# A hybrid encoder layer on one core: the gates of four heads and the forget logits of two heads computed as one more 2x2 block group

## The chip, the cores and the metric

The kernel runs on one core of one Trainium2 chip. The metric is the device time in microseconds. Five engines work side by side, each through its own queue of instructions in a fixed order, and they wait for each other by semaphores: TensorE (PE, matrix products), VectorE (DVE), ScalarE (ACT), GpSimd (POOL) and SyncE (SP, which issues most of the transfers). A matrix product reads its operands from the on-chip memory and adds into one of eight banks of 512 fp32 columns; DVE and ACT read those banks. An instruction that has to wait holds up everything behind it on its engine.

## The reference

One layer on x of 256 tokens by 2048 channels, all in fp32: half a feed-forward block, a mixer, half a feed-forward block. Only the mixer matters here:

```
h = rms_norm(x, pre_norm_mix)
q_h, i_h, f_fwd, f_bwd, g_h, q_a, k_a, v_a = split(h @ w_mix_in)  # 1024 columns each, k_a and v_a 256
qh, vh = heads(q_h), heads(i_h)                                   # 8 heads of 128
f = lb + (1 - lb) * sigmoid(heads(f_logit)); log_f, k = log(f), 1 - f   # forward, and backward flipped
o = chunk_scan(qh, k, vh, log_f)                                  # the two directions are added
y_h = o * rsqrt(mean(o * o) + EPS) * out_gain * silu(g_h)         # per head
y_a = window_attention(q_a, k_a, v_a, sink, rel_table)
x = x + rms_norm(concat(y_h, y_a) @ w_mix_out, post_norm_mix)
```

The columns of `w_mix_in` are, in this order, queries of the recurrence (0 to 1023), values (1024 to 2047), forward forget logits (2048 to 3071), backward forget logits (3072 to 4095), gates (4096 to 5119), queries of the attention (5120 to 6143), keys and values of the attention (6144 to 6655).

## The kernel before

**How fp32 products are made.** A weight tile is loaded from memory as a raw tile of 128 partitions by 2048 columns and split into halves of 1024 columns: ACT writes the rounded part `h` (line 177), DVE the remainder `l = raw - h` (line 178). The tokens `xt` have been split in the same way. A product in full precision is three passes on PE (line 458): `h` by high tokens, `l` by high tokens, `h` by low tokens. The tiles `h` and `l` come from two pools of five, so a new half can be written when PE is done with the half five before it. Three raw tiles are kept.

**Three forms of a projection.** *Values*: the 1024 value columns are a group of 2x2 blocks. `c` is four banks (token half m, column half n), and the 2048 input channels are eight pairs of 128. A plain pair takes eight products in three passes, 24 instructions. A pair of the class's table goes by seven products instead of eight (Strassen's scheme in Winograd's form): 21 instructions, into four further banks `p1, p5, p6, p7`, with sums of blocks made before. For the weights these sums are two accumulating transfers' work (issued by POOL, which adds block rows into the raw tile) and two DVE additions; for the tokens `sum_up` makes them. A raw tile of such a pair lies in one half of a room of its own, `vr`, and not in the three raw tiles. After the last mixed pair, `fold` adds the `p` banks into the `c` banks. *Gates* (`gates`, lines 379 to 381): 16 channel tiles by two token halves by three passes, 96 instructions of 512 columns per 512 gate columns. *Head pairs* (`headpair`, lines 326 and 331): 256 columns, weights stationary, so that the result stands with columns on partitions, which the recurrence needs: 32 instructions of 512 columns (high and low tokens at once) and 32 of 256 columns.

**The order.** Values, then for each pair of heads hp = 0 to 3: forward forget logits `zf`, backward `zb`, queries `q`, attention queries `qa`, each a `headpair`. The gates of heads 0 to 3 stand in hp = 1 between `zf` and `zb`. Small work of the recurrence and the attention is handed out between the pieces of the head pairs, by the generators in `side`: every `yield n` lets n pieces pass. Eight pieces are one half of a head pair. The values' part is written in a manual schedule: PE, DVE and ACT execute in the order of the text. Outside it a scheduler sets the order, by the text too, but with freedom.

Of the kernel before, what the change touches and what calls it, by code (L numbers as in the profile page):

```python
# [37 lines left out]
def hymba_layer_kernel(  # L38
# [380 lines left out]
    class Blocks:  # L419
# [52 lines left out]

        def one_block(self):
# [90 lines left out]
        def begin_next(self):  # L564

            if len(self.ahead) == 1:
                self.ahead.append(load(self.source(self.ahead[0])))
# [3 lines left out]
        def work(self, upto, among=None):  # L571


            while self.pos < upto:
# [8 lines left out]
                else:  # L583
# [4 lines left out]
                    else:  # L588
                        hs, ls = split_load(self.source(u))
# [983 lines left out]
    with ExitStack() as s2:  # L1573
# [40 lines left out]
        class Values(Blocks):  # L1614


            def __init__(self):
                super().__init__(
                    {u: pair_of(xt, u) for u in range(KT // 2)}, dict.fromkeys(VALUES)
                )  # L1620
                self.room = xp.tile([P, 2, 2048], F32, tag="X", name=nm("vr"))
                self.firsts = {}

            def source(self, u):
                return Pairs.part(w_in, u, 1)

            def left_sums(self, u):
                return self.sums[u]

            def raw(self, u):  # L1630
                return self.room[:, VALUES.index(u) % 2]

            def fetch(self, u):
                dst = self.raw(u).rearrange("p (k c) -> p k c", k=2)
                nc.sync.dma_start(dst, self.source(u))

            def prepare(self, u):

                raw = self.raw(u)
                tag = f"yt{6 + VALUES.index(u) % 2}"  # L1640
# [3 lines left out]
                nc.gpsimd.dma_start(  # L1644
                    raw[:, 0:1024].rearrange("p (k c) -> p k c", k=2),
                    self.source(u)[:, :, 512:1024],
                    accum_op=ALU.add,
                )

            def sum_up(self, u):  # L1650

                z, s = (
                    keepy.tile([P, 4, P], F32, tag=f"sy{i}", name=nm("vs"), bufs=1) for i in range(2)
                )
                x = self.tiles[u].bitcast(F32)
                whole = z.rearrange("p j t -> p (j t)").rearrange("p (k t) -> p k t", k=2)
                nc.vector.tensor_tensor(whole, x[:, :, 0, :], x[:, :, 1, :], ALU.add)
                tag = f"yt{(0, 1)[VALUES.index(u)]}"
                w = keepy.tile([P, 4, 2, P], F32R, tag=tag, name=nm("xs"), bufs=1)
                split_act(w[:, :, 0, :], w[:, :, 1, :], sums_of(whole, s))  # L1660
                self.sums[u] = w
# [547 lines left out]
```

## Time and profile before

| | us |
|---|---|
| median of three runs | 1817.84 (1817.8 to 1818.12) |
| the profiled execution | 1818.84 |
| its span, from the first to the last instruction | 1817.1 |
| mean granted TensorE clock | 0.999 |
| values, from the first product to the last | 729.6 to 771.9 |
| head pairs and gates, hp = 0 to 3 | 772.1 to 1034 |

The profiled execution takes 1.7 us more than its span and is 1.0 us over the median. Times in the views are from the start of the span. In a timeline a row is the start, the duration (the ends of matrix products are modelled and overlap the next), the engine, the line, out and in, the count, and in brackets how long the engine had been idle and what ended that.

### The profile page before, as it was taken

The numbers are of one execution on the slowest core, as the hardware profiler recorded it, in microseconds if no ns is written. First come the engines' busy times: TensorE is split into PE (matmuls) and PEld (weight loads), VectorE is DVE, ScalarE is ACT, GpSimd is POOL, SyncE is SP. The second block draws the span as 40 slices with busy tenths as digits, with TensorE's granted clock in tenths as the row PEclk, the third lists the DMA queues.
The fourth block names the chain that finished last, engine by engine and source line by source line (L and its number), as shares of the span: only waits on it lengthen the run. The fifth ranks groups of instructions, "written<-read, shape, count | busy, mean of one in ns | idle before, by whom it ended". The sixth has DMA issues, their size and how long they took to land.

```text
span 1817.1 us, 23612 instructions
## 1 busy us (share of the span) xinstructions
PE 1805.4 (99%) x8448; PEld 1501.9 (83%) x8448; DVE 1632.9 (90%) x2132; ACT 1143.1 (63%) x1519; POOL 164.4 (9%) x157
## 2 busy tenths in 40 slices
PE   9999999999999999999999999999999999999998
PEld 7888888888888888888888888888888888888886
DVE  7999999999989988987788898899999999999987
ACT  7566666666565757577587556556666666566663
POOL 1011111111011100000000000111111111011110
PEclk9999999999999999999999999999999999999999
DMA  8889999998699996766555456889999998699994
GB/s 303 237 234 283 276 283 255 255 256 259 215 344 276 281 321 228 243 203 181 170 163 162 164 208 245 251 244 267 283 272 269 259 246 248 192 342 307 265 317 159
DMA packets 211271, 452.85 MB, mean 249 GB/s; under 512 B 11865, under 2 KB 47025, under 8 KB 209873
## 3 DMA queue, kind: packets, MB, share of 16 engines
q1 hardware_dynamic: 178528, 389.06, 61.5%
q0 software_dynamic: 32448, 62.01, 19.9%
q8 instruction: 66, 1.08, 0.2%
q14 instruction: 53, 0.43, 0.1%
q10 hardware_dynamic: 176, 0.27, 0.0%
HBM read 436.60 MB, written 14.70 MB: 248 GB/s over the span
## 4 chain that ended last, share of the span: by engine, by line
PE 92%; DVE 4%; ACT 2%; DMA 2%; issue 1%; POOL 0%; DVEq 0%; ACTq 0%; POOLq 0%; SPq 0%
PE pa L458 41%; PE pb L458 36%; PE pa L326 5%; PE pa L331 3%; DVE l L178 2%; PE pa L381 1%; PE pa L380 1%; PE pa L379 1%; DMA raw<-in_w_ffn_gate_up_dram 1%; ACT h L177 1%; PE pb L1817 1%; PE pa L1169 1%; PE pb L1169 1%; PE pb L1929 0%; PE pb L1903 0%
## 5 line engine op out<-in xcount | busy, mean ns | idle before, releaser
L177 ACT CAST h<-raw 128x1024 fp32r<-128x1024 f32 (+1 forms) x863 | 849.9, 1012 | 452.7 <-PE pb L458 158.4
L178 DVE TENSOR_TENSOR l<-raw,h 128x1024 fp32r<-128x1024 f32 (+1 forms) x863 | 982.8, 1170 | 106.3 <-ACT h L177 80.1
L458 PE MATMUL pa<-h,xt 128*128 128x512 f32 x1148 | 403.3, 392 | 0.1
L458 PE MATMUL pb<-h,xt 128*128 128x512 f32 x992 | 355.3, 392 | 0.3 <-DVE pb L1226 0.3
L458 PEld LDWEIGHTS pa<-h,xt 128*128 128x128 f32 x1148 | 215.9, 188 | 46.1 <-DVE xt L233 0.6
L458 PE MATMUL pa<-l,xt 128*128 128x512 f32 x574 | 224.3, 391 | 0.0
L458 PEld LDWEIGHTS pb<-h,xt 128*128 128x128 f32 x992 | 186.5, 188 | 44.5 <-DVE pb L1233 3.7
L458 PE MATMUL pb<-l,xt 128*128 128x512 f32 x496 | 193.6, 390 | 0.0
L1008 POOL DMA_DIRECT2D raw<-in_w_ffn_gate_up_dram x78 | 94.6, 1212 | 733.6 <-DVE l L178 665.7
L458 PE MATMUL pb<-h,ht 128*128 128x512 f32 x452 | 159.3, 390 | 0.0
L458 PE MATMUL pa<-h,ht 128*128 128x512 f32 x452 | 159.3, 390 | 0.0
L458 PEld LDWEIGHTS pa<-l,xt 128*128 128x128 f32 x574 | 108.1, 188 | 21.3 <-DVE l L178 0.5
L326 PE MATMUL pa<-xt,h 128*128 128x512 f32 x512 | 123.6, 392 | 0.0
L458 PE MATMUL pa<-h,xs 128*128 128x512 f32 x320 | 114.5, 389 | 0.0
L458 PE MATMUL pb<-h,xs 128*128 128x512 f32 x320 | 111.5, 389 | 0.0
L326 PEld LDWEIGHTS pa<-xt,h 128*128 128x128 f32 x512 | 93.9, 188 | 18.0
L458 PEld LDWEIGHTS pb<-l,xt 128*128 128x128 f32 x496 | 93.4, 188 | 17.8
L458 PEld LDWEIGHTS pb<-h,ht 128*128 128x128 f32 x452 | 84.9, 188 | 17.5
L458 PEld LDWEIGHTS pa<-h,ht 128*128 128x128 f32 x452 | 84.9, 188 | 17.5
L458 PE MATMUL pa<-l,ht 128*128 128x512 f32 x226 | 88.0, 389 | 0.0
L458 PE MATMUL pb<-l,ht 128*128 128x512 f32 x226 | 88.0, 389 | 0.0
L1311 POOL DMA_DIRECT2D raw<-in_w_ffn_down_dram x38 | 46.1, 1212 | 371.2 <-DVE la L178 310.0
(327 smaller groups left out, 2545.0 us busy)
## 6 DMA issues: line engine op xcount, KB each, us to landing
raw<-in_w_ffn_gate_up_dram SPq DMA_DIRECT2D x350, 512.0 KB, 5.7
raw<-in_w_ffn_down_dram SPq DMA_DIRECT2D x88, 1024.0 KB, 7.8
raw<-in_w_mix_in_dram SPq DMA_DIRECT2D x50, 1024.0 KB, 5.1
raw<-in_w_ffn_gate_up_dram POOLq DMA_DIRECT2D x78, 512.0 KB, 8.0
raw<-in_w_ffn_down_dram POOLq DMA_DIRECT2D x38, 512.0 KB, 10.2
raw<-in_w_mix_out_dram SPq DMA_DIRECT2D x16, 1024.0 KB, 4.9
ht<-away SPq DMA_DIRECT2D x24, 512.0 KB, 10.5
away<-ht SPq DMA_DIRECT2D x16, 512.0 KB, 7.0
```

What stands on the lines that cost most here:

```text
L177: nc.scalar.copy(hi, src)
L178: nc.vector.tensor_tensor(lo, src, hi.bitcast(F32), ALU.subtract)
L326: nc.tensor.matmul(slot[f], weights(hs, kk, f), xcol(xt, k), start=(k == 0), stop=(k == KT - 1))
L331: nc.tensor.matmul(slot[f][:, 0:T], weights(ls, kk, f), xcol(xt, kh * 8 + kk, 0), start=False, stop=False,)
L379: nc.tensor.matmul(dst, xh, h[:, o : o + n], start=(k == 0), stop=False)
L380: nc.tensor.matmul(dst, xh, l[:, o : o + n], start=False, stop=False)
L381: nc.tensor.matmul(dst, xl, h[:, o : o + n], start=False, stop=(k == KT - 1))
L458: nc.tensor.matmul(self.bank(at), lhs, rhs, start=(n == 1), stop=n in (ends, self.of[at]), skip_group_check=n > ends,)
L1008: nc.gpsimd.dma_start(raw[:, 0:1024].rearrange("p (k c) -> p k c", k=2), self.source(u, g)[:, :, 1], accum_op=ALU.add,)
L1169: nc.tensor.transpose(bank[:, o : o + P], zs[m][:, k * P : (k + 1) * P], ident)
L1311: nc.gpsimd.dma_start(raws[i][:, 0:1024].rearrange("p (k c) -> p k c", k=2), Pairs.part(w_dn, u, r)[:, :, 512:1024], accum_op=ALU.add,)
L1817: nc.tensor.matmul(dst, left[a], right[b], start=first and i == 0, stop=last and i == 2)
```

## The change

The 512 gate columns of heads 0 to 3, the 256 forward and the 256 backward forget columns of heads 0 and 1 become one group of 1024 columns right behind the values, by the same class, now with a list of column ranges, an order of pairs and the pairs by seven as arguments. Its pairs come in the order 0, 1, 3, 2, 6, 4, 5, 7, those of channels 3, 6 and 5 by seven products. Pairs 3 and 6 use the token sums that the values made, pair 5 new ones. Each load becomes three transfers, each accumulation two. The result has tokens on partitions. The gates are used so; the forget logits (`zn`, after the sigmoid) are transposed on PE in eight transposes, eight pieces into `q` of hp = 0, and `hgrn_dir` reads them from the banks. The head pairs `zf` and `zb` of hp = 0 and the call of `gates(0)` go. The key transposes, so far among the pieces of `zf`, and the spreading of a scale over partitions stand between pairs 0 and 1 of the new group; the small work on lower bounds behind pair 1. The recurrence of hp = 0 is put off by eight pieces.

```diff
+            def fill(self, u, raw):
+                dst = raw.rearrange("p (k c) -> p k c", k=2)
+                at = 0
+                for c0, n in self.parts:
+                    src = w_in[u * 2 * P : (u + 1) * 2 * P, c0 : c0 + n]
+                    nc.sync.dma_start(
+                        dst[:, :, at : at + n], src.rearrange("(k p) c -> p k c", p=P)
+                    )
+                    at += n
...
             def prepare(self, u):
                 raw = self.raw(u)
-                tag = f"yt{6 + VALUES.index(u) % 2}"
+                tag = f"yt{6 + self.sevens.index(u) % 2}"
                 first = keepy.tile([P, 2, 512], F32R, tag=tag, name=nm("first"), bufs=1)
                 self.firsts[u] = first[:, 0], first[:, 1]
                 split_act(*self.firsts[u], raw[:, 0:512])
-                nc.gpsimd.dma_start(
-                    raw[:, 0:1024].rearrange("p (k c) -> p k c", k=2),
-                    self.source(u)[:, :, 512:1024],
-                    accum_op=ALU.add,
-                )
+                dst = raw[:, 0:1024].rearrange("p (k c) -> p k c", k=2)
+                at = -512
+                for c0, n in self.parts:
+                    if at >= 0:
+                        src = w_in[u * 2 * P : (u + 1) * 2 * P, c0 : c0 + n]
+                        nc.gpsimd.dma_start(
+                            dst[:, :, at : at + n],
+                            src.rearrange("(k p) c -> p k c", p=P),
+                            accum_op=ALU.add,
+                        )
+                    at += n
...
+            values = Columns([(1024, 512), (1536, 512)], range(KT // 2), (3, 6))
+            both = Columns(
+                [(4096, 512), (2048, 256), (3072, 256)], (0, 1, 3, 2, 6, 4, 5, 7), (3, 6, 5)
+            )
...
             values.work(5)
+            both.fetch(3)
             even(5, 6)
             values.work(6)
-            values.sum_up(6)
-            evened = even(7)
-            values.work(KT // 2)
+            sum_up(6)
+            even(7)
+            values.work(7)
+            raw = both.loaded(0)
+            both.fetch(6)
+            both.prepare(3)
+            values.work(KT // 2, lambda: first.append(split(raw)))
             for m in range(2):
                 for n in range(2):
                     nc.scalar.mul(
                         vh[:, m, n * 512 : (n + 1) * 512], values.c[m][n], rest[:, m : m + 1]
                     )
-        spread(rest)
-        with tc.issue_after(evened.ins):
+            both.start()
+            both.play(0, *first.pop())
+            both.pos = 1
+            spread(rest)
+            turned_keys()
+            both.work(2)
             lower_bounds()
+            both.prepare(6)
+            both.work(4)
+            both.fetch(5)
+            sum_up(5)
+            both.work(5)
+            both.prepare(5)
+            both.work(7)
+            both.work(KT // 2)
+            zn = mid.tile([P, 2, 512], F32, tag="sc", name="zn")
+            g = mid.tile([P, 2, 512], F32, tag="g", name="g")
+            for m in range(2):
+                by = rest[:, m : m + 1]
+                nc.scalar.activation(zn[:, m, :], both.c[m][1], AF.Sigmoid, scale=by)
+            for m in range(2):
+                by = rest[:, m : m + 1]
+                sl = both.c[m][0]
+                nc.scalar.activation(g[:, m, :], sl, AF.Sigmoid, scale=by)
+                nc.vector.scalar_tensor_tensor(g[:, m, :], sl, by, g[:, m, :], ALU.mult, ALU.mult)
+
+        def turn_z():
+            yield 8
+            for i, bank in enumerate((pa(), pb())):
+                for j in range(2):
+                    for m in range(2):
+                        o = i * 256 + j * P
+                        nc.tensor.transpose(
+                            bank[:, j * T + m * P : j * T + (m + 1) * P], zn[:, m, o : o + P], ident
+                        )
+                turned_z.append(bank.rearrange("p (j t) -> p j t", j=2))
+            yield 1
...
         for hp in range(4):
-            zf = headpair(2048 + hp * 256, "zf")
-            if hp == 1:
-                g = gates(0)
-                side.append(gated(*pending[0], g))
-            zb = headpair(3072 + hp * 256, "zb")
...
+            if hp:
+                zf = headpair(2048 + hp * 256, "zf")
+                if hp == 1:
+                    side.append(gated(*pending[0], g))
+                zb = headpair(3072 + hp * 256, "zb")
...
-            wait[0] = 0
+            wait[0] = 0 if hp else 8
```

Where the instructions stand shows at three places. In the names a number tells tiles of one kind apart, and the lines behind the change are those of the new file, some fifty to ninety further on.

The first is PE at the end of the values (before), where the spreading product is followed by the head pair `zf` and the key transposes come 28 products later:

```order
L458 MATMUL pb_6277<-l_6623,xt_5939 128x512
L458 MATMUL pb_6277<-h_6622,xt_5939 128x512
L291 MATMUL pb_6666<-R,ones 128x256
L326 MATMUL pa_6685<-xt_5938,h_6689 128x512
L326 MATMUL pa_6686<-xt_5938,h_6689 128x512
```

and PE behind pair 0 of the new group (now), where the halves of pair 1 are `h_6741`, `l_6742`:

```order
L458 MATMUL pb_6700<-h_6671,xt_5938 128x512
L291 MATMUL pb_6725<-R,ones 128x256
L1729 MATMUL pb_6730<-ident,kz 128x128 x4
L458 MATMUL pa_6697<-h_6741,xt_5938 128x512
L458 MATMUL pa_6697<-l_6742,xt_5938 128x512
```

The transposes have moved from the middle of a head pair to the row just ahead of pair 1's products.

The second is DVE at the same place. Before, five halves of the head pairs stand between the copy of the spread scale and the remainder of the keys (`low`):

```order
L296 COPY R<-pb_6666 128x256
L1605 TENSOR_SCALAR oml<-lb 128x16
L178 TENSOR_TENSOR l_6739<-raw_6736,h_6738 128x1024
L178 TENSOR_TENSOR l_6743<-raw_6736,h_6742 128x1024
L178 TENSOR_TENSOR l_6789<-raw_6786,h_6788 128x1024
L178 TENSOR_TENSOR l_6793<-raw_6786,h_6792 128x1024
L178 TENSOR_TENSOR l_6831<-raw_6828,h_6830 128x1024
L178 TENSOR_TENSOR low<-pb_6725,kT 128x512
```

Now (`l_6668` and `l_6672` are pair 0, `l_6742` and `l_6746` pair 1):

```order
L178 TENSOR_TENSOR l_6668<-raw_6627,h_6667 128x1024
L178 TENSOR_TENSOR l_6672<-raw_6627,h_6671 128x1024
L559 TENSOR_TENSOR pa_6276<-pa_6276,y_6650 128x512
L563 TENSOR_TENSOR pb_6277<-pb_6277,y_6651 128x512
L565 TENSOR_TENSOR pb_6278<-pb_6278,y_6651 128x512
L288 TENSOR_SCALAR R<-ident,scales 128x128 x2
L296 COPY R<-pb_6725 128x256
L178 TENSOR_TENSOR low<-pb_6730,kT 128x512
L178 TENSOR_TENSOR l_6742<-raw_6737,h_6741 128x1024
L178 TENSOR_TENSOR l_6746<-raw_6737,h_6745 128x1024
```

The remainder of the keys has moved ahead of both halves of pair 1, and no half stands between the copy and it.

The third is DVE at a fold. Before (the values' fold, with small work on the lower bounds between, and the first half of `zf`, `l_6690`, ahead of it):

```order
L178 TENSOR_TENSOR l_6623<-raw_6581,h_6622 128x1024
L1598 TENSOR_TENSOR e_6215<-cols,lbm 128x16
L1599 TENSOR_TENSOR e_6216<-cols,lbm 128x16
L178 TENSOR_TENSOR l_6690<-raw_6687,h_6689 128x1024
L546 TENSOR_TENSOR y_6626<-pb_6473,y_6626 128x512
L1602 TENSOR_TENSOR e_6216<-e_6215,e_6216 128x16
L539 TENSOR_TENSOR y_6627<-pb_6474,y_6626 128x512
L1603 RECIPROCAL e_6216<-e_6216 128x16
L540 TENSOR_TENSOR y_6626<-pa_6472,y_6626 128x512
L543 TENSOR_TENSOR y_6627<-pa_6472,y_6627 128x512
```

Now, from the second addition of pair 5 to the last row that reads its bank `p5` (`pa_6810`); `l_6957` and `l_6961` are pair 5, `l_6990` and `l_6994` pair 7, `l_7052` to `l_7094` the queries of hp = 0:

```order
L1684 TENSOR_TENSOR vr_6223<-vr_6223 128x512
L178 TENSOR_TENSOR l_6957<-vr_6223,h_6956 128x1024
L178 TENSOR_TENSOR l_6961<-vr_6223,h_6960 128x1024
L178 TENSOR_TENSOR l_6990<-raw_6985,h_6989 128x1024
L178 TENSOR_TENSOR l_6994<-raw_6985,h_6993 128x1024
L178 TENSOR_TENSOR l_7052<-raw_7049,h_7051 128x1024
L549 TENSOR_TENSOR y_6997<-pb_6811,y_6997 128x512
L178 TENSOR_TENSOR l_7056<-raw_7049,h_7055 128x1024
L542 TENSOR_TENSOR y_6998<-pb_6812,y_6997 128x512
L178 TENSOR_TENSOR l_7094<-raw_7091,h_7093 128x1024
L543 TENSOR_TENSOR y_6997<-pa_6810,y_6997 128x512
L546 TENSOR_TENSOR y_6998<-pa_6810,y_6998 128x512
```

Three halves of `q` have moved in front of and between the fold's rows.

More of the change, by code (lines that the diff above doesn't have):

```diff
@@ L471, in plain, with loaded @@
             self.three(("c", m, n), a[:, k, 0, ms], a[:, k, 1, ms], hs[k][:, cs], ls[k][:, cs])
+        def loaded(self, u):
+            return load(self.source(u))
         def one_block(self):
@@ L566, in begin_next @@
             if len(self.ahead) == 1:
-                self.ahead.append(load(self.source(self.ahead[0])))
+                self.ahead.append(self.loaded(self.ahead[0]))
             else:
@@ L588, in work @@
                     else:
-                        hs, ls = split_load(self.source(u))
+                        hs, ls = split(self.loaded(u))
                     self.play(u, hs, ls, among)
@@ L1716, in hymba_layer_kernel @@
             next_half(1)
-            values.begin(range(KT // 2))
-            raw = load(values.source(0))
+            values.start()
+            raw = values.loaded(0)
             values.fetch(3)
@@ L1748, in hymba_layer_kernel @@
             even(2, 3)
-            values.sum_up(3)
+            sum_up(3)
             values.work(4)
```

103 lines of the change are left out of this document (54 added, 49 removed).

## Prediction

> **What bounds the kernel now.** First the page's shares and its chain of work, then PE's waits, then the stretches around the change.
>
> ```profile
> PE 1805.4 (99%) x8448; PEld 1501.9 (83%) x8448; DVE 1632.9 (90%) x2132; ACT 1143.1 (63%) x1519; POOL 164.4 (9%) x157
> PE 92%; DVE 4%; ACT 2%; DMA 2%; issue 1%; POOL 0%; DVEq 0%; ACTq 0%; POOLq 0%; SPq 0%
> ```
>
> ```profile
> PE pb L1929 <- DVE at L1919: 0.6, 1, 0.6
> ...
> PE pb L1975 <- DVE on L1965: 0.4, 1, 0.4
> ```
>
> ```profile
> 740.00:760.00 20.00, 20.00 (x89) 16.37 (x88) 19.08 (x26) 11.28 (x13) 1.20 (x1) 1.00 0.68 197
> 760.00:775.00 15.00, 15.00 (x68) 12.44 (x67) 14.60 (x24) 12.01 (x16) 0.00 (x0) 1.00 0.70 247
> 775.00:796.00 21.00, 21.00 (x126) 18.71 (x126) 15.34 (x19) 14.93 (x21) 0.00 (x0) 1.00 0.69 225
> ```
>
> PE holds 92% of the chain, and in the mixer it waits for others only in these two rows, 1.0 us together. So a product less is its time less, and each wait added counts in full. The stretches (the first number behind the span is PE, the third DVE) show that in the values DVE works 19.1 of 20 us and PE still never waits: DVE is a step ahead. The head pairs leave DVE more room, 15.3 of 21.
>
> **Products removed and added.** Rows of PE; the first two from `gates(0)`; then the spreading product, the key transposes and two starts of a head pair's first half.
>
> ```profile
> 838.44 0.39 PE L379 MATMUL pa<-h,xt 128*128 128x512 f32 x1
> ...
> 843.20 0.39 PE L379 MATMUL pa<-h,xt 128*128 128x512 f32 x1
> ```
>
> ```profile
> 771.90 0.59 PE L291 MATMUL pb<-R,ones 128*128 128x256 f32 x2
> 772.14 3.99 PE L326 MATMUL pa<-xt,h 128*128 128x512 f32 x16
> ...
> 777.40 0.60 PE L1826 MATMUL pb<-ident,kz 128*128 128x128 f32 x4
> 777.76 0.72 PE L331 MATMUL pa<-xt,l 128*128 128x256 f32 x4
> ...
> 783.41 4.27 PE L326 MATMUL pa<-xt,h 128*128 128x512 f32 x18
> ...
> 794.54 4.27 PE L326 MATMUL pa<-xt,h 128*128 128x512 f32 x18
> ```
>
> 21 products lie between 838.44 and 843.20: 0.2267 us each. A head pair takes 794.54 - 783.41 = 11.13. Removed: two head pairs, 22.26, and 96 gate products, 21.76; together 44.02. Added: five plain pairs of 24 and three of 21, 183 products or 41.48, and eight transposes at 0.36 per four (777.40 to 777.76), 0.72; together 42.20. Net -1.8 us. The spread and key transposes only move. That is the whole gain: the forget columns would cost 96 products, 21.76, in the new form instead of 22.26, three pairs by seven save nine products, 2.04, and the transposes take 0.72 back.
>
> **The pause at pair 1.** I put the new group on the old clock: the values end at 771.90 as before, pair 0 at 777.34, the spread at 777.58 (0.24, as from 771.90 to 772.14) and the key transposes at 778.18 (0.60). Behind them PE needs pair 1. ACT must first copy the transposed keys out of the bank, then split pair 1; DVE must subtract the keys' remainder, then pair 1's.
>
> ```profile
> 729.78 0.47 ACT L1734 ACTIVATE kz<-pa,scales 128x256 f32<-128x256 f32 x1 [2.16 <-PE pa L381]
> ...
> 744.47 1.06 ACT L177 CAST h<-vr 128x1024 fp32r<-128x1024 f32 x1 [2.25 <-DVE vr L1670]
> ...
> 779.59 0.58 ACT L177 CAST kT<-pb 128x512 fp32r<-128x512 f32 x1
> ```
>
> ```profile
> 729.36 0.39 PE L381 MATMUL pa<-h,xt 128*128 128x512 f32 x1
> ```
>
> ```profile
> 738.46 0.69 DVE L178 TENSOR_TENSOR xs<-vs,xs 128x512 fp32r<-128x512 f32 x1 [0.69 <-ACT xs L177]
> ...
> 757.35 1.22 DVE L178 TENSOR_TENSOR l<-vr,h 128x1024 fp32r<-128x1024 f32 x1
> 758.49 0.28 DVE L288 TENSOR_SCALAR R<-ident,scales 128x128 f32<-128x128 f32 x1
> ...
> 780.86 0.68 DVE L178 TENSOR_TENSOR low<-pb,kT 128x512 fp32r<-128x512 f32 x1
> ```
>
> From PE's end (729.36 + 0.39) to ACT's start (729.78) pass 0.03 us; I take the same from ACT to DVE and back to PE. Keys on ACT from 778.21, pair 1's first half on ACT from 778.72 (the next cast starts some 0.06 before the end of the last) to 779.78, on DVE from 779.80 to 781.02. PE's second product goes at 781.05; unhindered it would go at 777.34 + 0.24 + 0.36 + 0.23 = 778.17. Cost 2.9 us, between 2.5 (the modelled end of the transposes lies early) and 3.1. Before, five halves already split stood between; that cover is gone. Worse, DVE stands before the copy of the spread scale from about 773.6, when fold and pair 0 are done, to 777.9: its lead is spent. From here DVE's rows go on one by one, a half at 1.14 (757.35 to 758.49): pair 1's other half, the lower bounds (about 1.5), pair 3's and 6's splits, two additions and four halves end at 790.2 with pair 3's last; PE, starting pair 3 at 786.3, asks for it sixteen products later, at 789.9. Cost 0.35 (0 to 0.6). DVE has some 36 us of rows in the group against PE's 42 (ten plain halves 11.4, three pairs by seven 16.0, the fold 4.8, small rows about 4), so afterwards it keeps up, without a lead.
>
> **The accumulation of pair 5.** The room for pair 5 is free after pair 3's last half, about 790.2; the load is there in time (6.1 us). But POOL's transfers wait for DVE's first split of it, which stands behind pair 2's half, the token sums (about 3.1) and pair 6 and ends at 800.2.
>
> ```profile
> 747.30 0.69 DVE L178 TENSOR_TENSOR first<-vr,first 128x512 fp32r<-128x512 f32 x1
> ...
> 758.68 0.69 DVE L1669 TENSOR_TENSOR vr<-vr 128x512 f32<-128x512 f32 x1
> 759.29 0.17 DVE L1597 TENSOR_TENSOR lbm<-cols 128x16 f32<-128x16 f32 x1
> 759.40 0.69 DVE L1670 TENSOR_TENSOR vr<-vr 128x512 f32<-128x512 f32 x1
> ```
>
> ```profile
> 731.02 1.23 POOL L1644 DMA_DIRECT2D vr<-in_w_mix_in_dram  x1 [8.55 <-DVE first L178]
> 748.40 1.20 POOL L1644 DMA_DIRECT2D vr<-in_w_mix_in_dram  x1 [16.15 <-DVE first L178]
> ```
>
> ```profile
> vr<-in_w_mix_in_dram POOLq DMA_DIRECT2D x1, 512.0 KB, 7.2
> ```
>
> ```profile
> vr<-in_w_mix_in_dram POOLq DMA_DIRECT2D x1, 512.0 KB, 5.8
> ```
>
> ```profile
> raw<-in_w_mix_in_dram SPq DMA_DIRECT2D x12, 1024.0 KB, 6.1
> ```
>
> POOL starts 0.4 us after the split (747.99 to 748.40), issues twice at 1.2, so the second transfer is issued at 801.8 and lands 5.8 to 7.2 us later (the two landings, the longer one among other traffic). I take 6.2, nearer the quiet one, as each is half the size: 808.0. DVE, done with pair 4 and pair 5's lower half at 803.5, waits for it, and behind that wait stand pair 5's upper and last halves, pair 7, three halves of `q` and the fold. With the two additions (0.72 and 0.60) and 1.22 more, PE's upper products can go at 810.6. PE starts pair 5 at 807.0 (pairs 2, 6 and 4 at 5.44, 4.76 and 5.44 from 791.4) and asks ten products later, at 809.3: 1.3 us (0 to 2.3).
>
> **The second bank of q.** `q`'s second product writes the bank `p5`, which DVE reads last in the last row of the third place of the change. The folds go at 0.60 each:
>
> ```profile
> 767.70 0.65 DVE L540 TENSOR_TENSOR y<-pa,y 128x512 f32<-128x512 f32 x1
> 768.26 0.68 DVE L543 TENSOR_TENSOR y<-pa,y 128x512 f32<-128x512 f32 x1
> ```
>
> Before, the fold was done at 768.9, three us ahead of PE. Now two additions (1.3), seven halves, three of them `q`'s (8.0), and four folds (2.4) lie between the landing and the end of that row: 819.8. PE, delayed so far, ends pair 7 at 818.5 and would write the bank at 818.7: 1.1 us (0.3 to 1.5).
>
> **What is free.** The eight transposes need `zn`. ACT reaches it behind the first cast of `qa`, whose load waits for pair 7's raw tile, freed at 814, and so lands at 820 (6.1); then a table load and two sigmoids:
>
> ```profile
> 785.46 1.28 ACT L2098 ACT_TABLE_LOAD   x1
> 786.75 0.63 ACT L2098 ACTIVATE zf<-zf 128x512 f32<-128x512 f32 x1
> ```
>
> so about 823.5, against PE's 826: 0 (to 1.0, since the 2 MB that come back into `X` when pair 5 frees the room now compete with that load). In hp = 0 DVE and ACT get the recurrence of two head pairs less time; the heads' products come eight pieces (5.6 us) into `zf` of hp = 1, by my walk 1.4 us after their inputs. In hp = 1 the side work loses the gates as cover and looks like the later hp, with the short waits quoted first: 0.4 (0 to 1.0). SP's 24 and POOL's 6 further issues hide: no row shows PE waiting for a load there.
>
> **Sum.** -1.8 + 2.9 + 0.35 + 1.3 + 1.1 + 0.4 = +4.25 us. The profiled execution, 1818.8, becomes 1823.1; it lies 1.0 above the median, 1817.84, which becomes 1822.1.
>
> **A rule against the change.** The clock of PE shows in its own spacing. At the kernel's start, behind small products with pauses:
>
> ```profile
> 9.09 0.63 PE L458 MATMUL pa<-h,xt 128*128 128x512 f32 x1
> 9.52 0.63 PE L458 MATMUL pb<-h,xt 128*128 128x512 f32 x1
> ...
> 10.52 0.39 PE L458 MATMUL pa<-h,xt 128*128 128x512 f32 x1
> ```
>
> 0.43 us per product, then 0.23. The Trainium skill, page "TensorE: Matmul & The Clock Gate", section "What's actually happening", says that a window of about 3.4 us without work halves the clock, and that as long a busy one restores it. By that rule the pause at pair 1, broken by one product (779.8), stays short of a window, and the sum holds; were it counted as one, the next products would run at half speed, which is the third rival.
>
> **Rivals.** *Pair 5 in time.* If its transfers land before 806.7 (both at under 4.9 us), the upper half is not late and the bank costs 0.35: -1.8 + 2.9 + 0.35 + 0.35 = +1.8, 1819.6, no slower than by 0.1%. For it speaks the half size, against it both landings quoted. *The gain stays.* Were every wait hidden, 1816.0; the order of rows speaks against it. *Clock.* The four products from 9.09 to 10.52 took 1.43 us instead of 0.91, 0.5 more; the slow stretch had begun before them, so I price it at up to three times that, +1.6, 1823.7. No row of the middle of the kernel shows it. *Recurrence of hp = 0.* If my walk through `q` and `qa` (22 us; eight casts at 1.05 and five table loads are 15 us of ACT alone) errs by 15%, 3.3 us less the reserve of 1.4: +1.9 and more, about 1824.6.
>
> **Chances.** Forecast 0.50 (1820.0 to 1824.5), pair 5 in time 0.25, gain stays 0.05, clock 0.06, recurrence 0.14. A measurement of this kernel can tell about 0.2%, 3.6 us, from no change: the bound is at 1821.5. A quarter of the forecast, all of pair 5 in time and of the gain lie within: 0.41; above it 0.57; under 1814.2 leads only an error in the counts: 0.02. The range 1818.6 to 1826.0 leaves out the full gain, and the sums in which several waits reach their upper ends.
>
> **What the profile of the changed kernel will show.** A row of PE's waits for `l` by line 178 of 2 to 3 us near 778; POOL's second transfer of pair 5 around 801 and DVE idle behind it; PE waiting for DVE at the first products of `q`; PE's instructions fewer by 33. I am wrong if PE goes through pair 1 without a stop, if DVE is not idle between 774 and 778, or if waits of hp = 0 and 1 outweigh these.

## The result, and the profile after

The changed kernel takes **1830.1 us** (median of six runs, 1829.0 to 1833.6) where the kernel before takes 1818.2 (1817.8 to 1819.1) beside it: a ratio of 1.0068, 95% interval 1.0056 to 1.0081. It is slower by 0.7%. The forecast was 1822.1 with a range up to 1826.0; the sign was right, and the time lies 4 us above the range. The profiled execution took 1831.95 us, 1.8 over the median, with a span of 1830.2 (13.1 more than before). What is read from traces below is one execution each; the medians are of several.

From the page: the shares and counts, and the shares of the chain.

```profile
PE 1809.1 (99%) x8415; PEld 1500.8 (82%) x8415; DVE 1647.0 (90%) x2151; ACT 1148.1 (63%) x1523; POOL 171.9 (9%) x163
PE 88%; DVE 5%; ACT 3%; DMA 2%; issue 1%; POOL 0%; DVEq 0%; SPq 0%; ACTq 0%; POOLq 0%
```

PE executes 33 products fewer, as counted, and yet 4 points of the chain have passed from PE to others. PE's waits, from 720 us to 1070 us (engine, tile and line, whom it waited for, us in total, times, the longest):

```profile
PE pb L1993 <- DVE at L1983: 3.2, 2, 2.7
PE pa L458 <- ACT h L177: 3.1, 2, 1.6
PE pa L458 <- DVE l L178: 1.8, 2, 1.0
PE pa L326 <- DVE y L546: 0.8, 1, 0.8
PE pb L1721 <- ACT pt L177: 0.5, 1, 0.5
PE pb L1721 <- DVE pl L178: 0.5, 1, 0.5
PE pb L2039 <- DVE on L2029: 0.4, 1, 0.4
```

Two rows have become seven. Rows two to four are the new group and the first products of `q`; the first row and the three last lie in hp = 1 and 2, in code that the change hardly touches. Three tiles of that code come up again: `at`, the masked scores that DVE makes for the head products of the recurrence; `kd`, an exponential of the recurrence; `pt` and `pl`, high and low part of the attention's transposed weights. In what follows a stop is priced by PE's starts: the distance of two starts less the usual one.

**At pair 1 and at pair 5.** PE's rows, then the rows of ACT and DVE that PE waits for.

```profile
777.70 0.60 PE L1729 MATMUL pb<-ident,kz 128*128 128x128 f32 x4
779.91 0.50 PE L458 MATMUL pa<-h,xt 128*128 128x512 f32 x1 [1.62 <-ACT h L177]
781.18 0.54 PE L458 MATMUL pa<-l,xt 128*128 128x512 f32 x1 [0.76 <-DVE l L178]
...
783.22 0.63 PE L458 MATMUL pb<-h,xt 128*128 128x512 f32 x1
783.65 0.63 PE L458 MATMUL pb<-l,xt 128*128 128x512 f32 x1
...
812.16 0.50 PE L458 MATMUL pa<-h,xs 128*128 128x512 f32 x1 [1.44 <-ACT h L177]
813.70 0.50 PE L458 MATMUL pa<-l,xs 128*128 128x512 f32 x1 [1.03 <-DVE l L178]
...
823.05 0.74 PE L326 MATMUL pa<-xt,h 128*128 128x512 f32 x2 [0.76 <-DVE y L546]
```

```profile
778.33 0.59 ACT L177 CAST kT<-pb 128x512 fp32r<-128x512 f32 x1 [4.22 <-PE pb L1729]
778.82 2.00 ACT L177 CAST h<-raw 128x1024 fp32r<-128x1024 f32 x2
...
778.95 0.69 DVE L178 TENSOR_TENSOR low<-pb,kT 128x512 fp32r<-128x512 f32 x1 [0.63 <-ACT kT L177]
779.89 1.23 DVE L178 TENSOR_TENSOR l<-raw,h 128x1024 fp32r<-128x1024 f32 x1 [0.25 <-ACT h L177]
...
802.87 1.22 DVE L178 TENSOR_TENSOR l<-vr,h 128x1024 fp32r<-128x1024 f32 x1
811.09 0.69 DVE L1683 TENSOR_TENSOR vr<-vr 128x512 f32<-128x512 f32 x1 [7.00 <-DMA vr<-in_w_mix_in_dram]
```

The stop at pair 1 costs 1.83 + 1.03 = 2.87 us, in two pieces with one product between. Behind it products start 0.43 us apart (783.22 to 783.65) instead of 0.23, eight of them: +1.6. At pair 5 DVE waits 7.0 us for the accumulated rows, and PE loses 1.60 + 1.31 = 2.9. `q` loses 0.92.

**The clock.** Stretches of 3.41 us, cut where the clock record changes and at whole multiples of that from there (behind the span: PE's busy time first; the clock third from the end).

```profile
778.09:781.51 3.42, 1.04 (x4) 0.48 (x3) 2.54 (x4) 3.16 (x4) 0.00 (x0) 1.00 0.00 0
781.51:784.92 3.41, 3.41 (x9) 2.63 (x8) 2.97 (x10) 2.94 (x6) 0.08 (x1) 0.50 0.42 90
808.81:812.22 3.41, 1.97 (x10) 1.32 (x8) 1.10 (x2) 1.05 (x1) 0.00 (x0) 1.00 0.46 125
812.22:815.63 3.41, 2.38 (x9) 1.73 (x10) 3.36 (x4) 3.02 (x4) 0.00 (x0) 1.00 0.00 0
962.41:965.82 3.41, 0.94 (x8) 0.74 (x7) 3.20 (x5) 3.12 (x6) 0.00 (x0) 1.00 0.72 230
965.82:969.24 3.42, 3.19 (x15) 3.19 (x16) 1.64 (x3) 0.00 (x0) 0.00 (x0) 0.50 0.13 33
```

The clock is exactly 0.50 for one such stretch, twice, each time behind a stretch in which PE worked about 1 us. The two stretches at pair 5 share about as much idle time (1.44 + 1.03) as the one at pair 1 holds alone (2.38); no half clock follows.

**At 963, far from the change.** The head products of hp = 2 wait 2.85 us for `at` where they waited 0.78 before, and the half clock behind them costs another 1.5. What is late there is a load of 1 MB: ACT waits for it, and DVE makes `at` behind ACT's cast and the remainder.

```profile
961.53 1.05 ACT L177 CAST h<-raw 128x1024 fp32r<-128x1024 f32 x1 [5.05 <-DMA raw<-in_w_mix_in_dram]
...
966.05 3.56 PE L1993 MATMUL pb<-vh,at 128*128 128x128 f32 x16 [2.69 <-DVE at L1983]
```

The transfer views, cut to the moment of issue, of before (945.0) and after (954.3):

```profile
raw<-in_w_mix_in_dram SPq DMA_DIRECT2D x1, 1024.0 KB, 5.0
```

```profile
raw<-in_w_mix_in_dram SPq DMA_DIRECT2D x1, 1024.0 KB, 7.1
```

and the queues in the 0.1 us from 956.2 of after:

```profile
q8 instruction: 1, 0.02, 86.2%
```

A transfer of instructions starts 1.9 us behind that load: one packet of 16 KB, which took 1.38 us (86.2% of 16 engines in 0.1 us). The records of single packets show, at the end of this load and the two behind it (965.0 to 966.5), 11 to 14 packets in each half microsecond where there had been some 170, of some 50 ns each (so nearly one after the other): I read that as one of the 16 DMA engines being late while the others are done. The records do not name the engine. Before, this queue's transfer started at 939.6, 5.4 us ahead of the load.

**The account**, in the profiled executions: products -1.8, pair 1 +2.87, half clock +1.6, pair 5 +2.9, `q` +0.92, the attention's products in hp = 1 +1.39, the head products of hp = 1 +0.70, those of hp = 2 +2.07 and +1.5 of half clock: 12.2 of 13.1 us. The rest was not placed. Both half clocks, 3.1 us, are of this one execution; run 8 shows that another need not have them.

### The profile page after: what moved, and what is told of

Same layout as the page of the kernel before. It is cut to its first block, busy times and chain, and to the rows that moved or that the text cites. A ratio compares the mean times of both kernels' runs of the same rounds, so it can differ in the third digit from the quotient of the medians.

```text
span 1830.2 us, 23637 instructions
## 1 busy us (share of the span) xinstructions
PE 1809.1 (99%) x8415; PEld 1500.8 (82%) x8415; DVE 1647.0 (90%) x2151; ACT 1148.1 (63%) x1523; POOL 171.9 (9%) x163
## 4 chain that ended last, share of the span: by engine, by line
PE 88%; DVE 5%; ACT 3%; DMA 2%; issue 1%; POOL 0%; DVEq 0%; SPq 0%; ACTq 0%; POOLq 0%
PE pa L458 42%; PE pb L458 37%; PE pa L326 3%; DVE l L178 3%; PE pa L331 1%; ACT h L177 1%; PE pa L381 1%; DMA raw<-in_w_ffn_down_dram 1%; PE pa L380 1%; PE pa L379 1%; DMA vr<-in_w_mix_in_dram 1%; DMA raw<-in_w_mix_in_dram 1%; PE pb L1172 1%; PE pa L1172 1%; PE pb L1993 1%
## 5 line engine op out<-in xcount | busy, mean ns | idle before, releaser
L458 PE MATMUL pa<-h,xt 128*128 128x512 f32 x1194 | 420.1, 393 | 1.8 <-ACT h L177 1.6
L458 PE MATMUL pb<-h,xt 128*128 128x512 f32 x1038 | 372.0, 393 | 0.0
L458 PEld LDWEIGHTS pa<-h,xt 128*128 128x128 f32 x1194 | 224.7, 188 | 50.0 <-ACT h L177 1.9
L458 PE MATMUL pa<-l,xt 128*128 128x512 f32 x597 | 233.4, 391 | 0.8 <-DVE l L178 0.8
L458 PEld LDWEIGHTS pb<-h,xt 128*128 128x128 f32 x1038 | 195.4, 188 | 46.5 <-DVE pb L1236 3.9
L458 PE MATMUL pb<-l,xt 128*128 128x512 f32 x519 | 202.5, 390 | 0.0
L326 PE MATMUL pa<-xt,h 128*128 128x512 f32 x448 | 108.8, 392 | 0.8 <-DVE y L546 0.8
L326 PEld LDWEIGHTS pa<-xt,h 128*128 128x128 f32 x448 | 81.9, 188 | 16.8 <-DVE y L546 1.2
```

Of the source, the lines that this page charges most:

```text
L326: nc.tensor.matmul(slot[f], weights(hs, kk, f), xcol(xt, k), start=(k == 0), stop=(k == KT - 1))
L458: nc.tensor.matmul(self.bank(at), lhs, rhs, start=(n == 1), stop=n in (ends, self.of[at]), skip_group_check=n > ends,)
```

## The experiments

All are timed against the kernel before; what a run changes is said against the changed kernel (1830.1, span 1830.2).

**1. Keys turned inside pair 0.**

```diff
-            both.play(0, *first.pop())
+            both.play(0, *first.pop(), lambda: (spread(rest), turned_keys()))
             both.pos = 1
-            spread(rest)
-            turned_keys()
```

> The spread product and the four key transposes go three places into pair 0 of the new group, so that 15 products of pair 0 (3.4 us) lie between them and pair 1. Theory (the stop behind the keys costs twice: 2.87 us of waiting, then 8 products at 0.427 instead of 0.227, 1.6 us): no wait at pair 1 over 0.4 us, no half-clock stretch near 781, some 4.5 us less than the changed kernel, about 1825.7. Rival (the time only moves: DVE is as late as before and the pair by seven or pair 5 waits in its place): the stop goes, but the waits at pair 3 or pair 5 grow by 2 us or more, and the time stays above 1828.

Measured: 1826.8 us, ratio 1.0048 (1.0033 to 1.0063). From 770 to 786 PE works all the time at full clock:

```profile
770.00:786.00 16.00, 16.00 (x74) 13.13 (x73) 13.81 (x24) 11.52 (x16) 2.45 (x2) 1.00 0.77 211
```

Between 771 and 786 PE gains 4.4 us on the changed kernel, the 2.87 and 1.6 of the account, and keeps 4.2 of it up to 830. The stops at pair 5 (1.82 + 1.31) and at 959 (2.84) stay. The profiled executions differ by 4.0, the medians by 3.4. The theory holds at its place.

**2. Eight products in the stop.**

```diff
             turned_keys()
+            both.p = [pa(), pa(), pb(), pb()]
+            for _ in range(8):
+                nc.tensor.matmul(
+                    both.p[0], pair_of(xt, 0)[:, 0, 0, 0:P], both.firsts[3][0], start=True, stop=True
+                )
             both.work(2)
```

> Eight products of 128x512 that nothing reads are put into the stop behind the key transposes (8 x 0.227 = 1.81 us, the first of the two gaps was 1.83). The wait for ACT and DVE stays as it is, PE only works in it. Theory (the half clock after the stop is set by how little PE did in it): the products of pair 1 go at 0.227 from the start, no half-clock record near 781, 1.6 us less than the changed kernel, about 1828.5. Rival (the slow products come from the halves of pair 1 being late, not from the clock): the same slow products, no gain, 1830.

Measured: 1828.1 us, 1.0056 (1.0041 to 1.0071). The first stretch is the one that held the stop; the two others lie at pair 5:

```profile
778.81:782.22 3.41, 2.65 (x12) 1.83 (x11) 3.10 (x4) 3.20 (x4) 0.00 (x0) 1.00 0.00 0
809.53:812.94 3.41, 0.71 (x3) 0.30 (x3) 2.64 (x4) 2.24 (x3) 0.00 (x0) 1.00 0.16 54
812.94:816.36 3.42, 3.42 (x9) 2.65 (x10) 3.42 (x4) 3.42 (x5) 0.00 (x0) 0.50 0.32 84
```

With work in the stop, the wait is the same and the half clock is gone; at 786 PE is 1.6 us ahead of the changed kernel, counted from 771. The products were slow by the clock, not by late halves. That the filling saved the clock is not shown by this run alone: the grid of stretches lies otherwise here than in the changed kernel, and without the eight products this one would have held about 1.6 us of work (an estimate: 2.65 less the 1.0 that they worked in it), between the values seen ahead of half stretches and of whole ones (last section). PE now reaches pair 5 1.1 us earlier, and the stretches lie 0.7 us later; so it waits 1.84 + 1.31 there within one stretch (busy 0.71 of 3.41), and loses the gain to a half clock. What the profiled execution gained came from 963: the load took 5.0 us, the stop 0.73, 3.6 us in all.

**3. The same stop, 1.6 us later.**

```diff
             both.start()
+            for _ in range(7):
+                nc.tensor.matmul(
+                    both.c[0][0], pair_of(xt, 0)[:, 0, 0, 0:P], both.firsts[3][0], start=True, stop=True
+                )
             both.play(0, *first.pop())
```

> Seven products that nothing reads stand ahead of pair 0 of the new group (1.59 us), so the stop of 2.9 us behind the key transposes is as long as before and starts 1.6 us later. In the changed kernel both half-clock stretches lasted 3.413 us and began at multiples of 3.413 us from one another (781.506, 965.825). Theory (fixed windows of 3.413 us, each judged by its own share of work): the stop now lies across two windows, each over 40% busy, and no half-clock stretch follows it: +1.6 - 1.6, 1830 as the changed kernel. Rival (any stop of about 2.9 us halves the clock): a half-clock stretch behind it, +1.6, about 1831.7.

Measured: 1830.6 us, 1.0067 (1.005 to 1.0083). The stop is the same, 1.83 + 1.03, and the clock stays whole:

```profile
778.00:781.42 3.42, 2.16 (x12) 1.62 (x10) 1.03 (x2) 1.22 (x2) 0.00 (x0) 1.00 0.00 0
781.42:784.83 3.41, 2.29 (x9) 1.67 (x10) 2.82 (x7) 2.92 (x6) 0.00 (x0) 1.00 0.00 0
784.83:788.24 3.41, 3.41 (x17) 2.83 (x16) 3.25 (x7) 3.31 (x4) 1.54 (x2) 1.00 0.88 277
```

The stretches lie as in the changed kernel here, within 0.1 us (778.00 against 778.09), so it is the stop that moved. At 786 PE stands where it stood in the changed kernel: seven products paid by the clock. So not the stop's length decides, but how it lies to fixed windows of 3.41 us. The load at 955 was fast here too (5.1 us, stop 0.82); this profiled execution gives 1.5 us of that back between 1700 and 1790, at a stop near 1761 in a later part, which was not followed.

**4. Pair 5's first split earlier.**

```diff
                 lower = split_half(raw, 1)
+                if self.also:
+                    self.also.pop()()
                 nc.vector.tensor_tensor(b22, b11, b22, ALU.add)
...
+            both.also.append(lambda: both.prepare(5))
             both.work(5)
-            both.prepare(5)
```

> The first split of pair 5, which releases POOL's accumulating transfers, moves from behind pair 6 to behind the lower half of pair 6 (its load landed at 796.4, that half ends at 796.2 on DVE): POOL issues some 3 us earlier, at about 797.5 and 798.3, ahead of the load of 1 MB that was issued at 802.98. Theory (the landing at 810.96 sets the stops of 1.60 and 1.31 us in pair 5, and the late fold the 0.92 at q): landing by 805, no stop in pair 5, at most 0.3 at q, some 3.5 us less than the changed kernel, about 1826.6. Rival (DVE itself is the limit there): DVE is no longer idle 7 us but PE still waits for its halves, less than 1.5 us gained. A price: pair 6's halves come 0.6 us later, with about 2 us of reserve.

Measured: 1826.9 us, 1.0048 (1.0033 to 1.0063). DVE goes on without a gap:

```profile
801.79 1.22 DVE L178 TENSOR_TENSOR l<-vr,h 128x1024 fp32r<-128x1024 f32 x1
803.04 0.69 DVE L1686 TENSOR_TENSOR vr<-vr 128x512 f32<-128x512 f32 x1
```

POOL issued at 796.27 and 797.00, the rows landed 4.5 and 5.65 us later, the last at 802.6. Between 786 and 860 PE has no wait left: 4.3 us gained there (2.9, 0.92, and less at small pieces). In the changed kernel the second transfer was issued at 801.82, as the forecast had it, and took 9.14 us: the load of 1 MB for `q`, issued at 802.98, was moved beside it and took 9.0 itself. In runs 1 to 3, with that load 1.2 us behind it, the transfer took 8.3, 8.4 and 7.8. Here the load was issued 4.9 us behind it, and took 4.8.

**5. All pairs plain.**

```diff
-                [(4096, 512), (2048, 256), (3072, 256)], (0, 1, 3, 2, 6, 4, 5, 7), (3, 6, 5)
+                [(4096, 512), (2048, 256), (3072, 256)], range(KT // 2), ()
...
-            both.fetch(3)
...
-            both.fetch(6)
-            both.prepare(3)
...
-            both.prepare(6)
...
-            both.fetch(5)
-            sum_up(5)
...
-            both.prepare(5)
```

> The new group without pairs by seven: eight plain pairs of 24 products in their plain order, no first splits, no accumulating transfers, no sums of tokens. 9 products more, +2.04 us. Theory (the accumulation of pair 5 costs 2.9 us in its stops and 0.92 at q, more than its pair saves): no stop between pair 2 and q, -3.8 + 2.0 = -1.8 against the changed kernel; 18 PE instructions more also shift PE's instruction fetch (next run but one), which took the 1 MB load of 954 from 5.0 to 7.1 us, -2.1 there and -2.3 of half clock: about 1824. Rival (DVE and ACT are just as short of time with plain pairs): stops of over 1 us in the second half of the group, 1828 or more.

Measured: 1826.3 us, 1.0039 (1.0024 to 1.0054). No stop from pair 2 to `q`; PE gains 2.2 us up to 830 (1.8 expected), although it has nine products more. At 963 it gains 3.7 (load 4.9 us, no half clock); a stop near 1759 takes 1.3 of that back. The time lies 2.3 above the expected 1824 and below the rival's 1828: the gain at 963 was 3.7 instead of 4.4, and the late stop was not foreseen. DVE and ACT are not short of time in plain pairs. As the changed kernel has them, the pairs by seven cost more in stops (3.8 us) than they saved in products (2.0).

**6. Runs 1 and 4 together** (both diffs).

> The edits of the first and the fourth run together: keys turned inside pair 0, pair 5's first split behind pair 6's lower half. The gains (1830.1 - 1826.8 and 1830.1 - 1826.9) lie at different places, so the theory has them add: 1823.5, with PE never waiting over 0.4 us between 760 and 870. The stop ahead of the head products near 955 stays (same instructions, so the same fetch of 16 KB behind the 1 MB load). Rival (one stop covers the other): over 1825.

Measured: 1823.3 us, 1.0022 (1.0012 to 1.0031), 0.2 from the sum. The gains add, and from 760 to 870 PE has no wait. The stop at 955 (2.84) is there with its half clock. Not in every execution, it seems: seven of the ten take 1822.7 to 1825.0, three 1819.8 to 1821.0, near the time of run 7; those three were not traced.

**7. Eight small products.**

```diff
-            both.play(0, *first.pop(), lambda: (spread(rest), turned_keys()))
+            def small_and_keys():
+                for _ in range(8):
+                    nc.tensor.matmul(
+                        both.c[1][1][:, 0:P],
+                        pair_of(xt, 0)[:, 0, 0, 0:P],
+                        both.firsts[3][0][:, 0:P],
+                        start=True,
+                        stop=True,
+                    )
+                spread(rest)
+                turned_keys()
+
+            both.play(0, *first.pop(), small_and_keys)
```

> As e6_keys_and_split, with eight products of 128x128 that nothing reads ahead of the key transposes (about 0.5 us, 16 PE instructions). In the changed kernel, and in the first and fourth run, a transfer of 16 KB of instructions started 2 us behind the load of 1 MB issued at 954.33 (950.59, 949.03), which took 7.1 us; in the second and third run, with eight and seven PE products more, it started 2.8 us ahead of that load, which took 5.0 us, and the stop at the head products was 0.7 to 0.8 instead of 2.85. Theory (that transfer is PE's own instruction fetch, and its place is set by the count of PE instructions): the fetch leaves the load, 5.0 to 5.1 us, stop 0.8, no half clock behind it: -2.1 - 2.3 + 0.5, about 1819.6. Rival (the load is slow for another reason, by chance of the run): no difference to e6_keys_and_split but +0.5.

Measured: 1820.1 us, 1.0012 (1.0003 to 1.0022): eight products more, and 3.2 us less than run 6. Stretches from 945 to 965 of run 6 and of this one:

```profile
945.00:965.00 20.00, 17.25 (x109) 15.82 (x109) 14.78 (x22) 6.52 (x12) 1.01 (x1) 0.91 0.65 212
```

```profile
945.00:965.00 20.00, 19.52 (x133) 17.72 (x132) 17.39 (x27) 10.11 (x24) 1.01 (x1) 1.00 0.79 237
```

In run 6 the transfer of instructions started at 948.43, 2.0 us behind the load, which took 7.1; here at 942.80, 3.0 us ahead of it, and the load took 4.9, the stop 0.60. The other instruction queue's transfer did not move (952.42 and 952.05). In the changed kernel from 795 to 1099 PE executed 1652 products and 1651 weight loads while that queue moved 13 transfers: 254 instructions each. So it is PE's own instructions, and 16 of them more went with a move of the transfer by 5 us against the load. The count alone does not make that: 16 instructions are 1.2 us at the rate of that place (265 in 20 us), and counted by the products and weight loads in the traces the transfer started at PE's instruction 8865 in run 6 (8863 in the changed kernel) and at 8823 here.

**8. Heads at once.**

```diff
-            wait[0] = 0 if hp else 8
+            wait[0] = 0
```

> The changed kernel with wait[0] = 0 behind hp = 0 too, as in the kernel before: the head products of heads 0 and 1 and the attention behind them start eight pieces earlier. Theory (the attention's cast of pt stands behind the kd row on ACT because the attention comes as late as that): the two stops at the products of pt and va (0.65 and 0.74 us near 883) go, and in their place PE waits ahead of the first head products near 848 by what the inputs are late, 5.6 us less the reserve of 1.4 that the prediction worked out, up to 4 us: 1830 to 1833. Rival (the inputs are ready early enough, the delay was never needed): no stop near 848 over 0.5 us, 1828.7.

Measured: 1830.4 us, 1.0068 (1.0052 to 1.0084), the time of the changed kernel. The stops at `pt` and `pl` are gone; in their place

```profile
848.70 0.94 PE L1967 MATMUL pb<-qd,kd 128*128 128x128 f32 x6 [2.22 <-DVE kd L1939]
```

The theory came: one stop of 2.2 us for two of 1.4 together. Without the eight pieces the inputs are late, with them the attention is.

This run shows something else. Its program is that of the changed kernel up to the heads, and PE's waits at pair 1 are the same (1.62 and 0.76), but in this execution they lie across two stretches, and the clock stays whole:

```profile
775.53:778.94 3.41, 1.95 (x11) 1.44 (x9) 1.12 (x2) 1.43 (x2) 0.00 (x0) 1.00 0.01 4
778.94:782.35 3.41, 2.50 (x10) 1.81 (x11) 2.91 (x7) 2.92 (x6) 0.00 (x0) 1.00 0.00 0
782.35:785.77 3.42, 3.42 (x17) 2.82 (x16) 3.28 (x7) 3.09 (x4) 1.76 (x2) 1.00 0.93 291
```

The half clock comes at pair 5 instead (last section). So the program does not fix where the stretches begin: one and the same stop costs its half clock in one execution and not in another. The six executions of the changed kernel fit that, though only one was traced: the mean clock is 0.998 in the fastest, 0.996 in the slowest, and one half stretch lowers it by 0.0009.

**9. The attention of heads 0 and 1 earlier, value products a piece later** (on run 7).

```diff
-            yield LAG_SOFTMAX if hp < 3 else LAG_LAST
+            yield (14, LAG_SOFTMAX, LAG_SOFTMAX, LAG_LAST)[hp]
...
-            yield LAG_AT
+            yield LAG_AT + (hp > 0)
```

> As e7_eight_small_products; in addition the transposes of the attention of heads 0 and 1 come 14 pieces behind their softmax instead of 22, and the value products of the heads one piece later in hp = 1 to 3 (6 instead of 5). Theory (what is left against the kernel before is the attention's cast of pt standing behind kd in hp = 1, 0.64 + 0.73, and the head products' wait for at, 0.68 and 0.60 in hp = 1 and 2): these four stops go, 2.6 us less at most, about 1817.6 to 1818.0, no different from the kernel before. Rival (ACT and DVE are short of time in hp = 1, so the stop only moves to another product): another stop of 1 us or more between 840 and 960, 1819.5 or more.

Measured: 1817.4 us, 0.9997 (0.9988 to 1.0006). PE's waits from 700 to 1080:

```profile
PE pb L2053 <- DVE on L2043: 0.4, 1, 0.4
PE pb L2007 <- DVE at L1997: 0.3, 1, 0.3
PE pa L458 <- DVE l L178: 0.2, 1, 0.2
```

The stops did not move elsewhere; the two edits were not tried apart. In the changed kernel ACT's cast of `pt` stood behind a table load and `kd`; eight pieces earlier it comes ahead of both. The rows of the changed kernel:

```profile
881.67 1.28 ACT L1937 ACT_TABLE_LOAD   x1
882.96 0.63 ACT L1937 ACTIVATE kd<-dm 128x512 f32<-128x512 f32 x1
883.50 1.05 ACT L177 CAST pt<-pb 128x512 fp32r<-128x512 f32 x2
```

**10. Run 9 without the eight small products.**

> As e9_attention_earlier, without the eight small products (0.5 us less, 16 PE instructions less). In e9 the 16 KB transfer of instructions started at 941.94, and in e6 (without the eight) it stood some 5 us later than in e7 (with them). Theory (the place of that transfer against the loads is set by the count of PE instructions): it moves to 946 to 947, beside the loads of 1 MB issued from 946.17, one of which takes 6.5 to 7.2 us instead of 5.5, and the stop at the head products near 952 grows from 0.43 to 1.5 us or more, with a half clock behind it if it fills most of a window: 1818.5 to 1821. Rival (the transfer doesn't come back to that place, or a stop there no longer depends on that load since the heads come a piece later): 0.5 us less than e9, 1816.9.

Measured: 1817.0 us, ratio 0.9990 (0.9981 to 0.9999). The rival came: 0.4 us less by the medians, 0.8 by PE's rows in the two traces (the two runs were timed on different chips). The transfer of instructions moved only 1.3 us against the loads (942.73 instead of 941.94, the loads 0.5 earlier), stayed 3 us ahead of the load of 945.69, and that took 5.4 us as in run 9. Here the transfer starts at the same count in both, PE's instruction 8835 and 8837, and 16 instructions are worth 1.3 us, as the rate of run 7 says; there the count itself jumped by 42. What makes it jump stays open. This is the fastest version, with all 33 products saved: 1.9 us under the kernel before as timed beside it (1818.95), 0.1%, less than the 0.2% that the forecast took a measurement to tell from no change.

## Why the prediction was wrong

**Right.** The net of the products: 33 fewer, and where the stops were removed down to two of 0.4 and 0.3 (run 10) PE gains 2.3 us on the kernel before between 771 and the end of the heads, -1.8 of it forecast and the rest, about 0.5, from stops that the kernel before had there. The pause at pair 1: +2.9 forecast, 2.87 found, in the forecast's order of ACT and DVE rows. The second transfer of pair 5 issued at 801.8: found at 801.82, with DVE idle behind it; the hit to the digit is luck, as the first was issued at 801.09, half a microsecond later than forecast, and the second only 0.73 behind it instead of 1.2. The bank of `q`: 1.1 forecast, 0.92 found. PE does not wait at the transposes of `zn`, and the recurrence of hp = 0 stops nothing. Pair 3's last half, +0.35, did not show; in runs 2 and 3, where the half clock is not there to delay PE, it did, with 0.40 and 0.39.

**Wrong, in the order of size.**

*A term that was missing: 3.6 us at 963.* The sum followed the change into hp = 1 and held hp = 2 to be as before. The failed step is the end of the sum: its last term is hp = 1, and what lies behind was put at nothing without a reason, though the wait of that place in the kernel before, 0.6 for `at`, is the first row that the forecast quotes. In the changed kernel PE's instruction transfer falls behind a load with no reserve; against that load it lies 7.3 us later than before, and 33 products at 0.2267 are 7.5. Run 7 shows the price: 16 instructions more, the transfer ahead of the load again, and the stop goes from 2.84 to 0.60 us. The clue stood in the chain of before, where that very load was followed by the head products without slack:

```profile
945.03 5.04 DMA raw<-in_w_mix_in_dram
...
954.69 2.05 PE pb L1929 x16
```

*"broken by one product, stays short of a window".* The clock rival, at 0.06, was what happened at pair 1, with the price it gave, +1.6; the price is right by luck, for it was taken as three times the half microsecond of another place and not from a stretch at half clock (3.41 us with 8 products for 15). The Trainium skill, page "TensorE: Matmul & The Clock Gate", section "What's actually happening", has a free-running window of about 3.4 us, an idle one of which halves the clock. The trace agrees on the length, 3.413, and runs 3 and 8 on the free-running. What the forecast made of "idle", no work at all, is what failed: a window with 1.04 us of work halved it, and in runs 5 and 8 one with 1.46; one with 1.88 (run 3) did not. Which stop meets such a window differs from execution to execution (run 8), and no profile of before could tell it.

*"I take 6.2, nearer the quiet one"*, in the accumulation of pair 5: +1.3 forecast, 2.9 found. The landing took 9.1 us. The forecast let `q`'s load arrive in time and did not ask what it does to the transfer beside it; run 4, which parts the two, has 5.65 and no stop.

*hp = 1, "looks like the later hp, 0.4 (0 to 1.0)"*: 2.1 found, 1.39 in the attention's products and 0.70 in the heads'. The second is like the later hp. The first is not: there `pt` does not meet `kd` on ACT, here it did, since the attention starts eight pieces later. Run 8, which takes the delay back, is without that stop; run 9 takes both away.

The forecast of +4.25 is thus 4.9 short in terms it had or named (clock 1.6, pair 5 1.6, hp = 1 1.7) and 3.6 in one it had not; pair 3 and the bank of `q` were 0.5 too high. That is the way from 4.25 to the 12.2 of the account.

## What to carry to other kernels

When PE is the bound, follow a change to the end of the stage behind it: its program is shorter, so every load without reserve meets other transfers, PE's own instructions among them. Price a stop with and without a half stretch behind it, since the phase is not yours to set, and ask for each late transfer what is issued a microsecond behind it. A form that saves an eighth of the products pays only if its preparation is released early: here moving one split (run 4) was worth 3.3 us, more than the 2.04 that the three pairs by seven saved.

## What the runs showed of the hardware that was not expected

- The half clock comes in whole windows of 3.413 us on a grid that runs through the execution. PE's work in the windows ahead of a half one, between pair 1 and hp = 2 in the changed kernel and runs 1 to 8: 0.71 (twice), 0.73, 0.94, 1.04, 1.13, 1.25 and 1.46 (twice) us of 3.41; ahead of whole ones that held a stop, the least: 1.88, 1.92, 1.95, 1.97. The border lies between 1.46 and 1.88. The windows below are of run 8, at pair 5. Where the grid lies against the program differs from execution to execution: at pair 1 a window begins at 778.09 in the changed kernel, at 778.94 in run 8, with the stop itself 0.8 us earlier there.

```profile
809.66:813.07 3.41, 1.46 (x5) 1.01 (x6) 3.33 (x4) 2.90 (x4) 0.00 (x0) 1.00 0.00 0
813.07:816.49 3.42, 3.42 (x10) 2.64 (x9) 3.42 (x4) 3.35 (x5) 0.00 (x0) 0.50 0.57 189
```

- PE's instructions come by transfers of 16 KB, one for about 254 of them on average (single distances from 197 to 300). Where one started 1.9 to 2.8 us behind this load of 1 MB, the load took 7.1 to 7.2 us instead of 5.0 (changed kernel, runs 1, 4 and 6); 1.0 behind, 5.9 (run 8); about 3 us ahead of it, 4.9 to 5.1 (runs 2, 3, 5 and 7).
- Idle time removed at one place can be lost at the next by phase alone: in run 2 most of the 1.6 us gained at pair 1 (1.2) were paid again up to 830, with a half clock at pair 5.
